# A hybrid encoder on one core: the low half of the attention keys above 64 rows of zeros

## The chip, the cores and the metric

The kernel runs on one core of one Trainium2 chip. The metric is the device time of one execution in microseconds (us). TensorE (PE in the rows) multiplies; its weight loads are listed apart (PEld). VectorE (DVE), ScalarE (ACT) and GpSimd (POOL) work element by element, SyncE (SP) and ScalarE issue transfers. The times before are the median of three runs.

## The reference

An encoder of four layers on 256 tokens of 1024 features, in float32. Each layer is a mixer and an MLP, each behind an RMS norm; the mixers are a state-space mixer (layers 0 and 3), a dilated attention (layer 1) and a differential attention (layer 2). What concerns the change are the attention scores, products of queries and keys over 64 features:

```python
# layer 1, three groups of window and dilation, 16 heads of 64 features
scores = jnp.einsum('brjqhe,brjkhe->brjhqk', qs, kb) / math.sqrt(hd)
scores = jnp.where(valid[:, None], scores + bias, NEG_INF)
...
# layer 2, 8 heads of two halves of 64 features; softmax of each, and their difference
logits = jnp.einsum('bqhie,bkhie->bhiqk', qb, k) + bias
a = jax.nn.softmax(logits, axis=-1)
attn = a[:, :, 0] - lam_full * a[:, :, 1]
```

## The kernel before

Tokens lie along the columns, features along the 128 partitions. Every float32 operand of a large product is split into a high half `hi`, rounded for TensorE's fast format, and a low half `lo`, the rest. A product is then the sum of three: hi x hi, hi x lo, lo x hi (`mm3`, lines 143 to 145). Weights stream from memory in chunks of 1024 columns; ScalarE makes `whi` (line 110) and VectorE `wlo` (line 112), some chunks ahead of their use.

Products over 64 features leave half of the partitions free. `mm2` (lines 128 to 131) uses that: `q` holds the queries' hi in partitions 0 to 63 and their lo in 64 to 127, `kh` holds the keys' hi twice, so that the first product gives hi x hi + lo x hi in one. The second product is hi x lo with the 64 rows of `kl`, the keys' lo:

```python
mm(out, lhsT=q, rhs=kh, start=start, stop=False, skip_group_check=True)
mm(out, lhsT=q[0:64], rhs=kl, start=False, stop=True, skip_group_check=True)
```

`split_keys` (lines 133 to 136) fills `kh` twice by ScalarE and `kl` by VectorE.

The dilated mixer (`dil_events`) runs over 8 head pairs. For each it projects queries and keys of three groups (`qk`), then the values (`vchunk`), and for two blocks of 128 queries makes the scores (`scores`), the transposes (`trans`) and the products with the values (`pv`). Only group 0 uses `mm2`, for the two heads of a pair in turn: four products for a pair and a query block. Groups 1 and 2 use `mm3` with 128 rows: their key tiles hold one head's 64 rows in each half of the columns and zeros elsewhere, written once by POOL.

The differential mixer (`diff_events`) runs over 4 pairs of heads: projections `q`, `k`, `v` (`proj`), then for each head and query block the scores of its two halves by `mm2`, again four products, the softmaxes and their difference `S` on VectorE and ScalarE, transposes (line 1016), the product with the values (line 1028, bank `a3`), a norm of the head whose result `o` is read out of that bank by VectorE (line 1035), and another transpose (line 1042).

Both mixers are lists of events with a time each; the program is emitted in the order of those times, and engines take their instructions in that order. At the start of a mixer stands the norm: POOL adds six of the squares (line 240), TensorE sums them over the features (line 268), in its queue between the first projections.

Of the kernel before, what the change touches and what calls it, by code (L numbers as in the profile page):

```python
# [10 lines left out]
F32 = mybir.dt.float32  # L11
F32R = mybir.dt.float32r
# [4 lines left out]
P = 128  # L17
T = 256
# [12 lines left out]
def classes(t):  # L31
    """Tokens j*4 + c of [.., 256] as [.., c, j]: the order of the dilated mixer."""
    return t.rearrange("p (j c) -> p c j", c=4)


class LayerPool:
    """The pool of the part that is being emitted."""
# [8 lines left out]
class Prog:  # L46
# [20 lines left out]
    @contextmanager  # L67
    def shifted(self, name):
        """Emits with the priority of a later (or earlier) place in the program."""
        n = max(self.tune[name], -self.tc.cur_priority)  # L70
        self.tc.cur_priority += n
        yield
        self.tc.cur_priority -= n

# [5 lines left out]
    def plan_chunk(self, key, ap):  # L80
        """A key that ends in "f32" is used as it is, without a split."""
        self.plan.append((key, ap))
# [44 lines left out]
    def mm2(self, out, q, kh, kl, start):  # L127
        """The product of 64 rows: q holds hi above lo, kh twice the keys' hi."""
        mm = self.nc.tensor.matmul
        mm(out, lhsT=q, rhs=kh, start=start, stop=False, skip_group_check=True)  # L130
        mm(out, lhsT=q[0:64], rhs=kl, start=False, stop=True, skip_group_check=True)  # L131
# [16 lines left out]
    def load(self, g, perm):  # L148
        """x to [feature, token] with the first gains, what the first products need ahead of the other constants."""
# [99 lines left out]
    def rsqrt(self, v, n):  # L249
        """1/sqrt(v) for v [128, n] (the guard within): a seed of the bits and two Newton steps, each with the factors that even its error out."""  # L250
        nc = self.nc
        t = lambda nm, dt=F32: self.ap_.tile([P, n], dt, tag=f"rs_{nm}_{n}", name=f"rs_{nm}_{n}", bufs=2)
        y, w, q = t("y"), t("w"), t("q", I32)
        nc.vector.tensor_scalar(out=q, in0=v.bitcast(I32), scalar1=-0.5, scalar2=float(0x5F1FFFF9), op0=ALU.mult, op1=ALU.add)
        cur = q.bitcast(F32)
        for a, b in ((0.703952253 * 2.38924456, 0.703952253), (1.5 * (1 + 3.17e-7), 0.5 * (1 + 3.17e-7))):
            nc.vector.scalar_tensor_tensor(out=w, in0=cur, scalar=-b, in1=cur, op0=ALU.mult, op1=ALU.mult)
            nc.vector.tensor_tensor(out=w, in0=w, in1=v, op=ALU.mult)
            nc.vector.scalar_tensor_tensor(out=y, in0=w, scalar=a, in1=cur, op0=ALU.add, op1=ALU.mult)
            cur = y  # L260
        return y

    def sums(self, bank, tiles, count):
        """bank [128 tokens, 2 blocks] = sums over the features of each [128 features, 256 tokens] over count, and eps."""
# [6 lines left out]
    def bcast_tok(self, r, scale, bank, out):  # L271
        """r [128 tokens, 2 blocks] times scale -> out [128, 256], the same on every partition."""
# [15 lines left out]
    def normalised(self, g_mix, perm=False, keep=False):  # L288
        """x*g/rms split, all of it."""
# [87 lines left out]
    def tail_chunks(self, key, w, k0, nk):  # L377
        """The last nk row blocks of an output product, cut by columns."""
# [3 lines left out]
    def proj_tail(self, acc, key, xs, finish, first=False):  # L382
        """The last row blocks of an output product, column block by column block."""
# [14 lines left out]
    def ssd_events(self, l, finish):  # L398
        """The layer as (time, weight chunks, emitter); a unit of time is one product of two column blocks."""
# [11 lines left out]
        def start():  # L411
            self.norm_finish("a0")
            st["n"] = self.normalised(gvec("g_mix", 8 * l, 8), keep=any(n[0] != "o" for n in cfg["native"]))
            # sums of squares of the gated y, two column blocks at a time
# [8 lines left out]
        def unit(kind, c0, defer):  # L423
            """Two column blocks of in_w from column c0; -> (bank, keys)."""
# [54 lines left out]
        # dt: softplus, its logarithm, sums along the tokens within the blocks of 128  # L479
# [12 lines left out]
        def dt_post():  # L492
# [24 lines left out]
            # ln(dt): a seed of the bits and Newton steps with exp  # L517
# [8 lines left out]
        def dt_sums():  # L526
            adt, ln = st["adt"], st["ln"]
            b = self.bank("r2")
            ge, le = self.C("tri_ge"), self.C("tri_le")  # [s, s']: 1 where s >= s', s <= s'
# [24 lines left out]
        def load_rows(g, i):  # L554
            """The rows of two heads on every partition."""
# [11 lines left out]
        def cb(g):  # L567
            b = self.bank("r2")
            B, C = st["B", g], st["C", g]
            for i in range(2):  # token blocks 1, 0  # L570
# [15 lines left out]
        def gh(g, i):  # L586
            """The decayed scores of two heads, [s, l] for both directions."""
            bc, tb = st["bc", g, i], st["tb"]
            X = lambda o, i_, bias: nc.scalar.activation(out=o, in_=i_, func=AF.Exp, bias=bias)  # L589
            # blocks of 128: [s1 l0 | s1 l1 | s0 l0 | s0 l1], then the forward diagonals of token blocks 1 and 0  # L590
# [15 lines left out]
        def y(g):  # L606
# [3 lines left out]
            # two heads in turn: they hold different columns of the array  # L610
# [40 lines left out]
        def r2():  # L651
            bank = self.bank("r2")
            # the sums are of 2y
# [52 lines left out]
    def bias_vectors(self):  # L706
        """[16 heads: by k-q from -256 | the same, far ones masked | by (k-q)/4 from -64 | the same, every fourth]."""
# [16 lines left out]
    def bias_rows(self):  # L724
        """Copies of the vectors one after another, of which a slanted pattern reads Toeplitz matrices."""
# [6 lines left out]
    def slanted(self, name, h, off, dims):  # L732
        """Row h of the vectors at off - step*i for each (step, count) of dims, and so on."""
# [4 lines left out]
    def split(self, hi, lo, src, scale):  # L738
        """hi + lo = src*scale, src in PSUM or SBUF."""
# [4 lines left out]
    def dil_events(self, l, finish):  # L744
# [9 lines left out]
        def start():  # L754
# [4 lines left out]
            for i in range(2):  # L759
                st["bias", i] = lp.tile([P, 2, 514], F32, name=f"bias{i}")  # L760
                nc.gpsimd.memset(st["bias", i][:, :, 258:514], -1e30)
                for g in range(1, 3):
# [14 lines left out]
        def qk(hp, g, defer):  # L777
# [15 lines left out]
            if g == 0:  # L793
                q, kh, kl = (lp.tile([P if i < 2 else 64, 2, T], F32R, tag=f"q0{i}", name=f"q0{i}", bufs=2) for i in range(3))
                for h in range(2):
                    r = slice(64 * h, 64 * h + 64)
                    self.split(q[0:64, h, :], q[64:128, h, :], src[r, 0, :], 0.125)
                    self.split_keys(classes(kh[0:64, h, :]), classes(kh[64:128, h, :]), classes(kl[:, h, :]), cj(src[r, 1, :]))
# [73 lines left out]
        def pv(hp, qb):  # L872
            """The two heads in turn: they hold different columns of the array."""
# [46 lines left out]
    def diff_events(self, l, finish):  # L920
# [8 lines left out]
        def start():  # L929
            self.norm_finish("a0")  # L930
            st["n"] = self.normalised(self.V("g_mix", 8 * l, 8))
            # -lambda on every partition; the gain of the head norm with its factor
# [7 lines left out]
            st["nlam"] = t[:, 4:5]  # L940
            nc.vector.tensor_scalar(out=t[:, 5:6], in0=self.V("subln", j), scalar1=1.0 - lam_init, scalar2=None, op0=ALU.mult)
# [8 lines left out]
        def proj(kind, p, defer):  # L950
# [34 lines left out]
            else:  # L985
                st["k", p] = []
                for s_ in range(2):
                    kh, kl = (lp.tile([n, 2, T], F32R, tag=f"k{s_}{n}", name=f"k{s_}{n}", bufs=2) for n in (P, 64))
                    self.split_keys(kh[0:64], kh[64:128], kl, src[64 * s_:64 * s_ + 64])
# [94 lines left out]
    def final_tile(self, n):  # L1084
        """A feature block of x*g, transposed."""
# [42 lines left out]
    def prepare_part(self, i):  # L1128
        """Plans the weights of a part; -> its emitter."""
# [49 lines left out]
def bucket(rel):  # L1179
    """The bucket of each distance (of the shapes alone)."""  # L1180
# [6 lines left out]
def prepare(nc, ins):  # L1187
    """The arrays of the launch: the inputs, laid out, and constants of the shapes alone."""
# [73 lines left out]
```

## Time and profile before

| | us |
|---|---|
| median of three runs | 1647.09 |
| the three runs | 1642.84, 1647.09, 1648.29 |
| span of the profiled execution | 1641.6 |
| dilated mixer within it | 437 to 736 |
| differential mixer within it | 915 to 1045 |

The span goes from the first to the last instruction of one profiled execution; a time of a run also holds what lies around it. Of the profiled execution only the span is recorded. The profile gives, for each engine, how long it was busy; for each stage the same; for each instruction its start and its duration. A matmul's start is observed, its end is modelled, and the next may start long before it.

### The profile page before, as it was taken

The numbers are of one execution on the slowest core, as the hardware profiler recorded it, in microseconds if no ns is written. First come the engines' busy times: TensorE is split into PE (matmuls) and PEld (weight loads), VectorE is DVE, ScalarE is ACT, GpSimd is POOL, SyncE is SP. The second block draws the span as 40 slices with busy tenths as digits, with TensorE's granted clock in tenths as the row PEclk, the third lists the DMA queues.
The fourth block names the chain that finished last, engine by engine and source line by source line (L and its number), as shares of the span: only waits on it lengthen the run. The fifth ranks groups of instructions, "written<-read, shape, count | busy, mean of one in ns | idle before, by whom it ended". The sixth has DMA issues, their size and how long they took to land.

```text
span 1641.6 us, 32376 instructions
## 1 busy us (share of the span) xinstructions
PE 1612.2 (98%) x13018; PEld 1552.6 (95%) x13018; DVE 1198.2 (73%) x1996; ACT 959.9 (58%) x1627; POOL 129.2 (8%) x116
## 2 busy tenths in 40 slices
PE   8999999999999999999999999999999999999998
PEld 7989999999999999999999999999999899899997
DVE  7999997555776666666556888755579999985554
ACT  5577865444666666655445666644455778654443
POOL 0011121000200000010000000100010231210001
PEclk9999999999999999999999999999999999999999
DMA  6677765766475555546665554566655777656651
GB/s 208 209 217 231 224 191 180 218 212 185 134 198 166 151 157 154 161 134 186 190 192 182 184 174 120 166 192 188 187 160 178 218 218 224 217 169 191 187 188 64
DMA packets 230294, 299.84 MB, mean 183 GB/s; under 512 B 16496, under 2 KB 166256, under 8 KB 230144
## 3 DMA queue, kind: packets, MB, share of 16 engines
q1 hardware_dynamic: 209552, 262.51, 52.4%
q10 hardware_dynamic: 20592, 35.27, 7.6%
q8 instruction: 102, 1.67, 0.4%
q14 instruction: 48, 0.39, 0.1%
HBM read 296.41 MB, written 3.62 MB: 183 GB/s over the span
## 4 chain that ended last, share of the span: by engine, by line
PE 79%; DVE 11%; DMA 4%; ACT 3%; issue 2%; POOL 0%; SPq 0%; DVEq 0%; ACTq 0%; POOLq 0%
PE r L143 14%; PE r L145 13%; PE r L144 13%; PE a L143 8%; PE a L145 8%; PE a L144 8%; DVE wlo L112 3%; DMA bc<-scr 2%; DMA raw<-in_ssd_in_w_dram 2%; PE r L141 1%; PE a L820 1%; PE r L614 1%; PE a L822 1%; PE a L821 1%; PE r L131 1%
## 5 line engine op out<-in xcount | busy, mean ns | idle before, releaser
L112 DVE TENSOR_TENSOR wlo<-raw,whi 128x1024 fp32r<-128x1024 f32 (+1 forms) x490 | 593.8, 1219 | 304.7 <-ACT whi L110 303.3
L110 ACT CAST whi<-raw 128x1024 fp32r<-128x1024 f32 (+1 forms) x490 | 502.6, 1032 | 458.1 <-PE r L144 237.6
L145 PE MATMUL r<-spl,wlo 128*128 128x256 f32 x1248 | 356.6, 286 | 3.7 <-DVE wlo L112 3.7
L143 PE MATMUL r<-spl,whi 128*128 128x256 f32 x1248 | 357.4, 287 | 0.5 <-ACT whi L110 0.5
L144 PE MATMUL r<-spl,whi 128*128 128x256 f32 x1248 | 357.3, 286 | 0.3 <-DVE spl L227 0.3
L143 PE MATMUL r<-nh,whi 128*128 128x256 f32 (+1 forms) x1024 | 290.1, 283 | 3.9 <-DVE cvx L469 2.4
L145 PE MATMUL r<-nh,wlo 128*128 128x256 f32 (+1 forms) x1024 | 285.0, 278 | 1.9 <-DVE wlo L112 1.9
L144 PE MATMUL r<-nl,whi 128*128 128x256 f32 (+1 forms) x1024 | 285.0, 278 | 0.0
L143 PE MATMUL a<-hh,whi 128*128 128x256 f32 x1024 | 283.2, 277 | 0.0
L144 PE MATMUL a<-hl,whi 128*128 128x256 f32 x1024 | 283.1, 276 | 0.0
L145 PE MATMUL a<-hh,wlo 128*128 128x256 f32 x1024 | 282.5, 276 | 0.0
L145 PEld LDWEIGHTS r<-spl,wlo 128*128 128x128 f32 x1248 | 242.1, 194 | 4.1 <-DVE wlo L112 3.9
L143 PEld LDWEIGHTS r<-spl,whi 128*128 128x128 f32 x1248 | 242.0, 194 | 1.1 <-ACT whi L110 0.7
L144 PEld LDWEIGHTS r<-spl,whi 128*128 128x128 f32 x1248 | 241.8, 194 | 0.9 <-DVE spl L227 0.5
L143 PEld LDWEIGHTS r<-nh,whi 128*128 128x128 f32 (+1 forms) x1024 | 192.3, 188 | 8.2 <-issue 3.6
L145 PEld LDWEIGHTS r<-nh,wlo 128*128 128x128 f32 (+1 forms) x1024 | 192.4, 188 | 2.8 <-DVE wlo L112 2.1
L144 PEld LDWEIGHTS r<-nl,whi 128*128 128x128 f32 (+1 forms) x1024 | 192.4, 188 | 0.7 <-DVE nl L300 0.2
L143 PEld LDWEIGHTS a<-hh,whi 128*128 128x128 f32 x1024 | 192.4, 188 | 0.2 <-ACT whi L110 0.2
L144 PEld LDWEIGHTS a<-hl,whi 128*128 128x128 f32 x1024 | 192.4, 188 | 0.0
L145 PEld LDWEIGHTS a<-hh,wlo 128*128 128x128 f32 x1024 | 192.2, 188 | 0.0
L240 POOL TENSOR_TENSOR sqacc<-sqacc,sq 128x256 f32<-128x256 f32 x48 | 43.5, 906 | 1129.5 <-ACT sq L238 1126.2
L589 ACT ACTIVATE e<-bc,tb 128x256 f32<-128x256 f32 (+1 forms) x256 | 95.6, 447 | 1.9 <-DVE bc L564 1.4
(250 smaller groups left out, 2421.7 us busy)
## 6 DMA issues: line engine op xcount, KB each, us to landing
raw<-in_mlp_w_dram SPq DMA_DIRECT2D x256, 512.0 KB
raw<-in_ssd_in_w_dram SPq DMA_DIRECT2D x96, 512.0 KB
bc<-scr ACTq DMA_DIRECT2D x32, 768.0 KB
raw<-in_dil_qkv_w_dram SPq DMA_DIRECT2D x48, 512.0 KB
raw<-in_ssd_out_w_dram SPq DMA_DIRECT2D x32, 512.0 KB
raw<-in_dil_qkv_w_dram SPq DMA_DIRECT2D x64, 192.0 KB
raw<-in_diff_qkv_w_dram SPq DMA_DIRECT2D x24, 512.0 KB
raw<-in_dil_out_w_dram SPq DMA_DIRECT2D x8, 512.0 KB
```

The source lines that it names most:

```text
L110: self.nc.scalar.copy(out=hi[:, :n], in_=raw[:, :n])
L112: self.nc.vector.tensor_tensor(out=lo[:, :n], in0=raw[:, :n], in1=hi[:, :n].bitcast(F32), op=ALU.subtract)
L131: mm(out, lhsT=q[0:64], rhs=kl, start=False, stop=True, skip_group_check=True)
L141: mm(out, lhsT=wh, rhs=xh, start=start, stop=stop, skip_group_check=True)
L143: mm(out, lhsT=wh, rhs=xh, start=start, stop=False, skip_group_check=True)
L144: mm(out, lhsT=wh, rhs=xl, start=False, stop=False, skip_group_check=True)
L145: mm(out, lhsT=wl, rhs=xh, start=False, stop=stop, skip_group_check=True)
L240: nc.gpsimd.tensor_tensor(out=self.sqs[0], in0=self.sqs[0], in1=sq, op=ALU.add)
L589: X = lambda o, i_, bias: nc.scalar.activation(out=o, in_=i_, func=AF.Exp, bias=bias)
L614: nc.tensor.matmul(b[(h % 2) * 64:(h % 2) * 64 + 64, n * T:(n + 1) * T], lhsT=xt[:, 1 - i, h * 64:(h + 1) * 64], rhs=G[h][:, i * T:(i + 1) ...
L820: mm(o, lhsT=nh[:, k, t], rhs=w_h, start=k == 0, stop=False)
L821: mm(o, lhsT=nh[:, k, t], rhs=w_l, start=False, stop=False)
```

## The change

The low half of the keys becomes a tile of 128 partitions of which the lower 64 (64 to 127) are zeros, and the second product of `mm2` takes all 128 rows of `q`: q.hi x k.lo + q.lo x 0. The zeros are written once, by POOL, when the mixer starts. So these tiles can't come from a rotating tag any more: the dilated mixer has two standing ones (head pairs alternate), the differential mixer four (two halves, pairs alternate). Before, each had two buffers to a tag, of the same columns.

```diff
@@ mm2
-        mm(out, lhsT=q[0:64], rhs=kl, start=False, stop=True, skip_group_check=True)
+        mm(out, lhsT=q, rhs=kl, start=False, stop=True, skip_group_check=True)
+
+    def lo_keys(self, name):
+        t = self.lp.tile([P, 2, T], F32R, name=name)
+        self.nc.gpsimd.memset(t[64:128].bitcast(F32), 0.0)
+        return t
@@ dil_events, start, for i in range(2)
+                st["kl", i] = self.lo_keys(f"kl{i}")
@@ dil_events, qk
-                q, kh, kl = (lp.tile([P if i < 2 else 64, 2, T], F32R, tag=f"q0{i}", name=f"q0{i}", bufs=2) for i in range(3))
+                q, kh = (lp.tile([P, 2, T], F32R, tag=f"q0{i}", name=f"q0{i}", bufs=2) for i in range(2))
+                kl = st["kl", hp % 2]
...
-                    self.split_keys(classes(kh[0:64, h, :]), classes(kh[64:128, h, :]), classes(kl[:, h, :]), cj(src[r, 1, :]))
+                    self.split_keys(classes(kh[0:64, h, :]), classes(kh[64:128, h, :]), classes(kl[0:64, h, :]), cj(src[r, 1, :]))
@@ diff_events, start
+            for i in range(4):
+                st["kl", i] = self.lo_keys(f"kl{i}")
@@ diff_events, proj
-                    kh, kl = (lp.tile([n, 2, T], F32R, tag=f"k{s_}{n}", name=f"k{s_}{n}", bufs=2) for n in (P, 64))
-                    self.split_keys(kh[0:64], kh[64:128], kl, src[64 * s_:64 * s_ + 64])
+                    kh, kl = lp.tile([P, 2, T], F32R, tag=f"k{s_}", name=f"k{s_}", bufs=2), st["kl", 2 * (p % 2) + s_]
+                    self.split_keys(kh[0:64], kh[64:128], kl[0:64], src[64 * s_:64 * s_ + 64])
```

The rest of the difference takes comments and docstrings out, which shifts line numbers: from `mm3` on, a line has 6 more (line 143 becomes 149), and in the differential mixer 10 more (line 1035 becomes 1045).

On TensorE, the first scores of the dilated mixer before. `r` is the bank of group 0 and then that of groups 1 and 2; of the names behind the arrow the first is the streamed operand, `q_5317` the queries' tile, `q_5318` and `q_5319` the keys' hi and lo, which shared its naming:

```order
L145 MATMUL r_5559<-nh,wlo 128x256
L130 MATMUL r_5635<-q_5318,q_5317 128x256
L131 MATMUL r_5635<-q_5319,q_5317 128x256
L130 MATMUL r_5635<-q_5318,q_5317 128x256
L131 MATMUL r_5635<-q_5319,q_5317 128x256
L143 MATMUL r_5636<-k_5219,q_5393 128x256
```

The same place on TensorE after:

```order
L151 MATMUL r_5562<-nh,wlo 128x256
L130 MATMUL r_5637<-q_5322,q_5321 128x256
L131 MATMUL r_5637<-kl_5219,q_5321 128x256
L130 MATMUL r_5637<-q_5322,q_5321 128x256
L131 MATMUL r_5637<-kl_5219,q_5321 128x256
L149 MATMUL r_5638<-k_5221,q_5396 128x256
```

Nothing moved here: the second product reads another tile, and its rows, which this list doesn't show, are 128 where they were 64.

On POOL, from the last memsets of the dilated mixer over the sums of squares that follow (those of four norms in one row) to the last state-space mixer, before:

```order
L766 MEMSET k_5239 64x256
L765 MEMSET k_5240 64x256
L766 MEMSET k_5240 64x256
L240 TENSOR_TENSOR sqacc<-sqacc,sq 128x256 x24
L600 TENSOR_TENSOR e<-e 128x2x256 x5
```

and after:

```order
L772 MEMSET k_5244 64x256
L773 MEMSET k_5244 64x256
L246 TENSOR_TENSOR sqacc<-sqacc,sq 128x256 x11
L136 MEMSET kl_10952 64x512
L136 MEMSET kl_10954 64x512
L136 MEMSET kl_10956 64x512
L136 MEMSET kl_10958 64x512
L246 TENSOR_TENSOR sqacc<-sqacc,sq 128x256 x13
```

The four memsets of the differential mixer stand ahead of the last of the six adds of its norm. In the dilated mixer's start two memsets of 64x512 join those that stood there, and the last add there has moved up by one place among them: one 64x512 and four 64x256 stand between the first memset of `bias` and it, where six 64x256 stood.

## Rows read from the trace of the kernel before

**Rows 1.** The page's first part: busy time of each engine, its share of the span, its instructions.

```profile
PE 1612.2 (98%) x13018; PEld 1552.6 (95%) x13018; DVE 1198.2 (73%) x1996; ACT 959.9 (58%) x1627; POOL 129.2 (8%) x116
```

**Rows 2.** Busy time by stage, the dilated and the differential mixer. Columns: from and to, length, then busy time (and instructions) of PE, PEld, DVE, ACT and POOL, the granted clock of PE, the busy share of the DMA engines and GB/s.

```profile
437.00:736.00 299.00, 297.77 (x2352) 283.49 (x2352) 204.65 (x431) 189.17 (x333) 9.17 (x16) 0.99 0.55 155
915.00:1045.00 130.00, 129.59 (x1001) 120.90 (x1000) 109.17 (x318) 88.51 (x200) 5.55 (x6) 1.00 0.50 152
```

**Rows 3.** Whom TensorE waited for, from 430 to 736 us and from 905 to 1045 us: us in total, times, the longest.

```profile
PE a L268 <- POOL sqacc L240: 2.4, 1, 2.4
PE r L143 <- DVE q L136: 1.2, 1, 1.2
...
PE a L937 <- DVE lamt L935: 1.7, 1, 1.7
PE a L1042 <- DVE o L1035: 0.4, 2, 0.2
PE a L268 <- POOL sqacc L240: 0.3, 1, 0.3
```

**Rows 4.** The 64-row products of line 131, by their operands (`q,q` in the dilated, `k,q` in the differential mixer), with the least, median and greatest duration in ns, the first and the last start; and the group of 128-row scores of line 144 in the dilated mixer, with its busy time and mean ns.

```profile
L131 PE MATMUL r<-q,q x32: 379/382/382, 469.1 to 698.6; 64*128 64x256 f32 x32
L131 PE MATMUL r<-k,q x32: 380/383/384, 935.4 to 1008.9; 64*128 64x256 f32 x32
...
L144 PE MATMUL r<-k,q 128*128 128x256 f32 x32 | 9.0, 282 | 0.0
```

**Rows 5.** TensorE's timeline at a score of the dilated mixer: start, duration, line, tiles, rows*columns of the weights, the streamed operand.

```profile
468.79 0.28 PE L145 MATMUL r<-nh,wlo 128*128 128x256 f32 x1
468.91 0.28 PE L130 MATMUL r<-q,q 128*128 128x256 f32 x1
469.12 0.38 PE L131 MATMUL r<-q,q 64*128 64x256 f32 x1
469.43 0.38 PE L130 MATMUL r<-q,q 128*128 128x256 f32 x1
469.74 0.38 PE L131 MATMUL r<-q,q 64*128 64x256 f32 x1
470.06 0.39 PE L143 MATMUL r<-k,q 128*128 128x256 f32 x1
470.28 0.28 PE L144 MATMUL r<-k,q 128*128 128x256 f32 x1
470.39 0.28 PE L145 MATMUL r<-k,q 128*128 128x256 f32 x1
470.51 0.28 PE L143 MATMUL r<-k,q 128*128 128x256 f32 x1
```

**Rows 6.** The same at eight score products of the differential mixer, the first two, the last, and what follows.

```profile
982.37 0.28 PE L130 MATMUL r<-k,q 128*128 128x256 f32 x1
982.58 0.38 PE L131 MATMUL r<-k,q 64*128 64x256 f32 x1
...
984.45 0.38 PE L131 MATMUL r<-k,q 64*128 64x256 f32 x1
984.76 0.44 PE L1042 MATMUL a<-head,o 128*128 128x128 f32 x2
```

**Rows 7.** POOL's timeline at the start of the dilated and of the differential mixer: start, duration, what; in brackets the idle time ahead.

```profile
433.20 0.52 POOL L761 MEMSET bias<- 128x512 f32 x1
433.66 0.30 POOL L765 MEMSET k<- 64x256 f32 x1
434.00 0.31 POOL L766 MEMSET k<- 64x256 f32 x1
...
435.76 0.82 POOL L240 TENSOR_TENSOR sqacc<-sqacc,sq 128x256 f32<-128x256 f32 x1
...
906.86 1.94 POOL L240 TENSOR_TENSOR sqacc<-sqacc,sq 128x256 f32<-128x256 f32 x2 [1.61 <-ACT sq L238]
910.41 1.19 POOL L240 TENSOR_TENSOR sqacc<-sqacc,sq 128x256 f32<-128x256 f32 x1 [1.60 <-ACT sq L238]
```

**Rows 8.** Busy time of two head pairs of the differential mixer, columns as in rows 2.

```profile
941.90:966.50 24.60, 24.60 (x191) 22.54 (x190) 19.72 (x60) 17.33 (x40) 0.00 (x0) 1.00 0.59 176
966.50:991.10 24.60, 24.60 (x191) 22.54 (x190) 21.58 (x71) 17.64 (x42) 0.00 (x0) 1.00 0.57 176
```

**Rows 9.** Timelines of VectorE and TensorE where bank `a3` is used again: VectorE's reading of one head (two instructions), then the first product of the next.

```profile
974.98 0.61 DVE L1035 TENSOR_SCALAR o<-a,rs_y 128x128 f32<-128x128 f32 x2
...
976.01 1.05 PE L1028 MATMUL a<-v,PT 128*128 128x128 f32 x8
...
999.35 0.60 DVE L1035 TENSOR_SCALAR o<-a,rs_y 128x128 f32<-128x128 f32 x2
...
1000.72 0.49 PE L1028 MATMUL a<-v,PT 128*128 128x128 f32 x3
```

**Rows 10.** Busy time by stretch as in rows 2, ahead of the first projections of the dilated mixer and behind: the granted clock is the number behind POOL's.

```profile
433.50:437.00 3.50, 0.87 (x6) 0.67 (x6) 3.47 (x6) 2.03 (x4) 3.18 (x10) 1.00 0.36 103
438.00:441.60 3.60, 3.60 (x19) 3.60 (x19) 2.83 (x10) 1.05 (x1) 2.19 (x8) 0.53 0.23 58
```

## The prediction

> **What bounds the kernel now.** I read the busy time by engine first: TensorE is busy 98% of the 1641.6 us span, VectorE 73%, ScalarE 58%, POOL 8% [rows 1]. That is an average over nine stages, so next I cut the two stages that the change touches out of it. The dilated mixer lies between 437 and 736 us, the differential mixer between 915 and 1045 us. In the first TensorE is busy 297.8 of 299 us and VectorE 204.7; in the second TensorE is busy 129.6 of 130 us and VectorE 109.2, which is 84% and much closer [rows 2]. The list of waits says the same: TensorE stands still for 3.6 us (2.4 and 1.2) around the first and 2.4 us around the second, most of it at their starts (the sum of squares, the factor lambda), and none of it at a score [rows 3]. So both mixers are as long as TensorE's row of products, and a product that starts sooner moves all that follows. But a busy TensorE is not yet a TensorE at its pace, since the ends of products are modelled. What counts is the time from one start to the next, which only the timeline shows.
>
> **The products of the scores.** A score takes two products, one with 128 rows (line 130) and one with 64 rows (line 131); there are 64 of the second, 32 in each mixer, recorded at 0.38 us each, where the 128-row product of the same block of scores (line 144) is recorded at 0.28 us [rows 4]. The starts in the dilated mixer tell more [rows 5]. Before the scores, starts lie 0.12 us apart (468.79, 468.91). Then the distances are 0.21 to the first 64-row product, 0.31, 0.31 and 0.32 from one to the next, and 0.22 even from the first 128-row product behind them to the second. After that it is 0.11 or 0.12 again. From 468.91 to 470.28 five distances take 1.37 us. It is not the 64-row product alone that is slow: the 128-row product of line 130 that stands between two of them starts 0.31 late as well, and so does the first product behind them. Each change between 64 and 128 rows costs, in both directions. In the differential mixer the scores of two query blocks often stand in one row of eight, from 982.37 to 984.76: 2.39 us for eight distances [rows 6].
>
> The control for "after" stands in the same rows: lines 143 to 145 `r<-k,q` are scores too, with 128 rows of which half are zeros in the keys, the same shape of 256 columns and the same kind of output. They start 0.115 to 0.12 us apart. The first and second of them (lines 143 and 144) share their weights as the two products of line 130 and 131 do, so that repeated weights are no cost either.
>
> **The change part by part.**
>
> *The product with 128 rows.* With kl 128 rows tall nothing changes its row count any more. Dilated mixer: 1.37 - 5 x 0.117 = 0.785 us for each of 16 blocks (8 head pairs x 2 query blocks), 12.6 us. Differential mixer: 2.39 - 8 x 0.117 = 1.45 us for a row of eight, which is two of its 16 blocks; 8 x 1.45 = 11.6 us. Gross gain 24.2 us. Bounds: nothing at all, if the new products keep 0.31 us, and 24.2 us.
>
> *What takes it back in the dilated mixer.* TensorE being sooner helps only if its inputs are there. Each score still precedes its own softmax, so VectorE and ScalarE are also released sooner; VectorE is busy 68% and ScalarE 63% there [rows 2], and only 0.785 us of some 19 us (299 / 16) are taken out. I take 0, at most 3 us.
>
> *What takes it back in the differential mixer.* Here two head pairs take 49.2 us, with VectorE busy 19.7 + 21.6 = 41.3 us [rows 8]. Four rows of eight fall into that time, so TensorE would want 4 x 1.45 = 5.8 us less, 43.4 us, and VectorE would be 95% busy. The narrow place is the output bank a3: the product of line 1028 must wait until VectorE (line 1035) has read the head before. At 976.01 that reading has been over for 0.42 us (974.98 + 0.61), at 1000.72 for 0.77 us (999.35 + 0.60) [rows 9]. In both cases a row of eight scores lies between the bank's filling and this reuse, so TensorE arrives 1.45 us sooner, and VectorE's part between is a chain that the scores hardly start: TensorE waits about 1.0 and 0.7 us. At the mixer's end, where the last heads run out and no projection is left to hide them, I add 0.6 us by the same reasoning (an estimate from these two rows). Together 2.3 us. Bounds: 0, and 11.6 us if VectorE's present idle time is all latency that can't shrink.
>
> *The memsets.* Six rectangles of 64x512 zeros are added on POOL. A memset of 64x256 takes 0.30 us with the next start 0.35 later, one of 128x512 takes 0.52 with the next 0.46 later [rows 7], so I bound one by 0.35 and 0.52. In the differential mixer all four stand between the fifth and the sixth add of the sum of squares; POOL is free there from 908.80 to 910.41, 1.61 us [rows 7], against 1.4 to 2.1 us for the four. The sixth add starts between 0 and 0.5 us later, and TensorE, which waited 0.3 us for it [rows 3], may wait that much more; I take 0.2. What the first memset waits for are tiles of earlier stages whose readers have long finished. In the dilated mixer the opposite happens: ahead of the sixth add stood six memsets of 64x256 (433.66 to 435.76, 2.10 us), and now stand one 64x512 and four 64x256, 1.75 to 1.9 us. TensorE waits 2.4 us for that add [rows 3], so 0.2 to 0.3 us come back. The two cancel: 0.
>
> *Nothing else moves.* The other engines' orders are as before except for the name of the written tile. The low halves are written by the same VectorE instruction with the same 64 rows, and two (four) standing tiles alternate as the two buffers of each tag did. Weight loads have the same 128 columns.
>
> Sum: 24.2 - 2.3 = 21.9, rounded to 22 us. The profiled execution has a span of 1641.6 us, so its span should become about 1619.6. The median of the three runs, 1647.1 us, lies 5.5 us above that span and the fastest run 1.2 us; I keep the 5.5 and predict 1647.1 - 22 = 1625.1 us.
>
> **The rivals.**
>
> *Nothing is taken back.* VectorE's chains are started by the scores and come sooner by as much. For it: the narrow places are few. Against: 0.42 and 0.77 us of room for 1.45. Then 1647.1 - 24.2 = 1622.9.
>
> *VectorE becomes the bound of the differential mixer.* For it: 84% busy, 95% wanted. Against: its work for weights runs many products ahead, so it has a reserve, and the stage has only four head pairs to use it up. Then only 12.6 us remain: 1634.5.
>
> *The product isn't shortened.* If the 0.31 us belonged to the second use of the array for a score, whatever its rows, nothing would be gained and the time would be 1647. Against it stands the control of [rows 5]: 128-row scores with half their keys zero at 0.12 us. The Trainium skill, page "TensorE: Matmul & The Clock Gate", section "Why this matters for your kernels", says that a single product with few rows takes the same time as one with 128; by that rule alone rows of zeros buy nothing and the sum is 0. The page "TensorEngine Tiling (Array Packing)", section "Key Properties", says that a change of the tiling mode drains the array, without a price; by that, the sum is the one above. From the rows alone: 0.31 us stand only on either side of a 64-row product, 0.12 us between 128-row products of scores, so I leave this rival little.
>
> *Slower: the clock.* Place: the differential mixer's reuse of a3, once per head. When TensorE had been busy only 0.87 of 3.5 us ahead of 437.0, the granted clock stood at 0.53 in the following 3.6 us [rows 10], that is mostly at 1.2 GHz of 2.4, which costs about 1.7 us beside the wait of 2.4 us [rows 3]. If TensorE came to wait as long for VectorE at a head, that head would cost 4.1 us. From six of eight heads on the change is a loss (24.6 against 24.2 us); with all eight, 32.8 us, the time is 1655.7. Against: I expect waits of 1 us, two of them.
>
> **How the numbers follow.** My forecast, part of the gain taken back, 0.57: 1625.1. Nothing taken back 0.25: 1622.9. VectorE bounds the second mixer 0.11: 1634.5. Not shortened 0.05: 1647. Slower by the clock 0.02: 1655.7. The range takes in the first two with the scatter of the runs, which lie 4.3 us below and 1.2 us above their median, and up to some 8 us taken back: 1619 to 1633. A difference under 0.3%, 5 us, can't be told from no change. Faster by more than that 0.93, within it 0.05, slower 0.02.
>
> **What would show it.** In the new profile, the starts around lines 130 and 131 should lie 0.115 to 0.12 us apart with no slow product behind them, and both forms should be recorded at 0.28 us. The dilated mixer should be some 12 us shorter, the differential one some 9. TensorE should show new waits for VectorE's line 1035 (now 1045), of about 1 us, and its wait for the sum of squares should shrink a little in the dilated and grow a little in the differential mixer. I am wrong if the starts keep 0.31 us, or if TensorE's new waits in the differential mixer add up to more than 5 us.

## The result and the profile after

The changed kernel takes 1625.1 us (median of four executions, 1624.6 to 1627.2), the kernel before 1645.0 (four executions, 1641.0 to 1648.3, the three that were known among them). The ratio is 0.9883, with a 95% interval from 0.9866 to 0.9899: 1.2% or 19.8 us faster. Forecast were 1625.1 us, and 22 us less than before. The agreement to 0.1 us is partly luck: the median of before came out 2.1 us lower, and the gain 2 us smaller. The span of the profiled execution, forecast at 1619.6 us, is 1625.4 us: the 5.5 us between a span and the median that the forecast carried over didn't come back.

The busy times by engine are the answer to [rows 1]. TensorE lost 17.7 us of busy time with as many instructions; POOL has the six memsets more.

```profile
PE 1594.5 (98%) x13018; PEld 1550.6 (95%) x13018; DVE 1194.8 (74%) x1996; ACT 959.2 (59%) x1627; POOL 132.9 (8%) x122
```

TensorE's timeline at the score of [rows 5], after:

```profile
466.07 0.28 PE L151 MATMUL r<-nh,wlo 128*128 128x256 f32 x1
466.19 0.28 PE L130 MATMUL r<-q,q 128*128 128x256 f32 x1
466.30 0.28 PE L131 MATMUL r<-kl,q 128*128 128x256 f32 x1
466.42 0.28 PE L130 MATMUL r<-q,q 128*128 128x256 f32 x1
466.54 0.28 PE L131 MATMUL r<-kl,q 128*128 128x256 f32 x1
466.65 0.28 PE L149 MATMUL r<-k,q 128*128 128x256 f32 x1
466.77 0.28 PE L150 MATMUL r<-k,q 128*128 128x256 f32 x1
```

Every distance is 0.11 or 0.12 us; from the first product of the score to the second behind it (466.19 to 466.77) five distances take 0.58 us, where they took 1.37. The row of eight of [rows 6], its first two products, the last, and what follows:

```profile
969.88 0.28 PE L130 MATMUL r<-k,q 128*128 128x256 f32 x1
970.00 0.28 PE L131 MATMUL r<-kl,q 128*128 128x256 f32 x1
...
970.72 0.28 PE L131 MATMUL r<-kl,q 128*128 128x256 f32 x1
970.84 0.38 PE L1052 MATMUL a<-head,o 128*128 128x128 f32 x2
```

0.96 us for eight distances, where it was 2.39. All 64 products are now as in the group of line 131 (answering to [rows 4]; least, median, greatest in ns):

```profile
L131 PE MATMUL r<-kl,q x64: 274/282/363, 466.3 to 991.1; 128*128 128x256 f32 x64
```

Both mixers by windows between the same products as in [rows 2], columns as there:

```profile
433.40:727.40 294.00, 290.26 (x2352) 284.26 (x2353) 204.65 (x431) 189.47 (x333) 10.34 (x19) 0.98 0.56 158
907.10:1026.80 119.70, 118.11 (x999) 117.09 (x999) 108.12 (x317) 87.58 (x200) 5.56 (x6) 0.99 0.55 165
```

The differential mixer is 10.3 us shorter, the dilated only 5.0, though its 16 blocks of scores gave what was forecast. The list of TensorE's waits there (answering to [rows 3]; us in total, times, longest) shows the largest part of what took it:

```profile
PE r L149 <- DVE kl L142: 3.7, 1, 3.7
PE a L274 <- POOL sqacc L246: 2.4, 1, 2.4
...
PE a L1038 <- DVE o L1045: 1.1, 2, 0.7
PE a L1052 <- DVE o L1045: 0.4, 2, 0.2
PE a L274 <- POOL sqacc L246: 0.2, 1, 0.2
```

TensorE waited 1.2 us for the low half of the keys in the first head pair, and now waits 3.7. (The product that waits is a projection: its bank `r` is free only when VectorE has made `kl` out of it. This is called the wait for the low keys from here on.) TensorE's timeline at that wait (idle time ahead in brackets), and the window of what follows, with the granted clock behind PE to POOL:

```profile
472.89 0.28 PE L151 MATMUL r<-nh,wlo 128*128 128x256 f32 x1
476.91 0.55 PE L149 MATMUL r<-nh,whi 128*128 128x256 f32 x1 [3.74 <-DVE kl L142]
477.26 0.42 PE L150 MATMUL r<-nl,whi 128*128 128x256 f32 x1
477.48 0.41 PE L151 MATMUL r<-nh,wlo 128*128 128x256 f32 x1
```

```profile
476.10:482.90 6.80, 5.99 (x28) 6.02 (x29) 3.38 (x7) 3.67 (x9) 0.00 (x0) 0.50 0.76 218
```

A product starts 0.21 us behind the last instead of 0.12: the clock stands at 0.50, that is 1.2 GHz, for 6.8 us. Behind the same wait of before it stood at 1.00:

```profile
478.00:485.00 7.00, 7.00 (x55) 6.48 (x56) 4.45 (x9) 4.66 (x9) 0.00 (x0) 1.00 0.69 194
```

Both kernels have the same products in the same order on TensorE, so each start can be set against its like. The table is worked out from the starts of the two profiled executions (us):

```
before   after    difference  place
 429.1    425.4    -3.7       ahead of the dilated mixer
 465.4    462.7    -2.7       ahead of its first score
 481.9    483.6    +1.8       behind the wait and the slow clock
 707.4    698.8    -8.6       behind its last score
 897.1    888.4    -8.6       ahead of the differential mixer
 927.9    920.6    -7.3       ahead of its first score
1013.3    995.1   -18.2       behind its last score
1200.0   1181.9   -18.2       ahead of the next mixer
1227.1   1210.5   -16.6       behind its start
1621.4   1605.2   -16.2       at the end
```

Each of the 16 blocks of the dilated mixer takes 0.78 us off the difference, and the differential mixer 10.9 us in all. In between, the steps upwards are the first head pair (+5.3 with its one block of -0.8 counted apart: 2.5 of wait, 2.8 of slow clock), three stage starts (+1.0, +1.3, +1.6) and some 1.3 us within the dilated mixer: from 481.9 to 707.4 us 15 blocks should give 11.7 us, and the difference moves by 10.4. These are lost, 0.4 us each, in three stretches of projections that hold no wait (502 to 515, 567 to 581 and 633 to 646 us of before): equal products with 128 rows start 0.114 us apart there before, and 0.118 after. At the three stage starts the clock fell in both kernels, for 3.4 us in this execution of before and for 6.8 in this one of after; the table's first line, 3.7 us ahead of anything that was changed, is scatter of the same kind the other way. So one pair of traces gives the mechanism; the size of the whole has to come from medians, and that of a stretch without such a start from several profiles.

### The profile page after: what moved, and what is told of

The parts are those of the page before. It is cut to its first block, busy times and chain, and to the rows that moved or that the text cites. A ratio compares the mean times of both kernels' runs of the same rounds, so it can differ in the third digit from the quotient of the medians.

```text
span 1625.4 us, 32385 instructions
## 1 busy us (share of the span) xinstructions
PE 1594.5 (98%) x13018; PEld 1550.6 (95%) x13018; DVE 1194.8 (74%) x1996; ACT 959.2 (59%) x1627; POOL 132.9 (8%) x122
## 4 chain that ended last, share of the span: by engine, by line
PE 80%; DVE 10%; DMA 4%; ACT 3%; issue 2%; POOL 0%; SPq 0%; DVEq 0%; ACTq 0%; POOLq 0%
PE r L149 14%; PE r L151 14%; PE r L150 14%; PE a L149 8%; PE a L150 8%; PE a L151 8%; DVE wlo L112 3%; PE r L147 2%; DMA raw<-in_ssd_in_w_dram 2%; PE a L829 1%; PE a L828 1%; PE a L830 1%; DMA bc<-scr 1%; PE r L620 1%; PE a L887 1%
```

## The experiments

My theory: what is slow is a change between 64 and 128 rows, and it costs 0.785 us a block in the dilated mixer and 0.725 in the differential (half of 1.45). Rivals: a 64-row product is slow by itself; the new tiles and memsets have a part in it. On the missing part of the dilated mixer there were two theories: that sooner scores meet VectorE's unchanged chain (the gain turns into the wait), and that the weights of that stretch came late in this execution, whatever the scores.

**The kernel once more.** No edit. From here on, a time is a median, and stands against executions of before on the same chip.

> The changed kernel as it is, a second time. In its profile the first head pair of the dilated mixer waited 3.7 us for VectorE's kl (1.2 us in the kernel before) and the granted clock then stood at half for 6.8 us; at three stage starts it stood at half for 6.8 us where the kernel before had 3.4. Theory: the gain of the scores is fixed (24 us), and what is taken back in the dilated mixer hangs on how late the weights of the first head pair arrive, so that it differs from run to run: a gain of 18 to 22 us again, and a wait of 1 to 4 us at that place. Rival: the wait and the fall of the clock belong to the changed order of POOL and to the sooner scores, and come back in the same size and at the same place in every profile.

1626.4 us against 1645.5, ratio 0.9887 (0.9864 to 0.9910). The gain repeats: 19 to 20 us. The wait for the low keys was 3.5 us and the clock fell behind it again, for 3.4 us.

**Short product.** The tall tiles and the memsets stay, the second product reads 64 rows of them:

```diff
-        mm(out, lhsT=q, rhs=kl, start=False, stop=True, skip_group_check=True)
+        mm(out, lhsT=q[0:64], rhs=kl[0:64], start=False, stop=True, skip_group_check=True)
```

> The changed kernel with its second product taken back to 64 rows; standing tiles and memsets stay. Theory: tiles and memsets cost nothing, so the time is that of the kernel before, within 2 us, and the starts at the scores are 0.21, 0.31, 0.31, 0.32 and 0.22 us apart again. Rival: the memsets on POOL cost time at the two norms, 0.5 to 2 us above the kernel before.

1643.1 us against 1645.5, ratio 0.9985 (0.9972 to 0.9998). Without the 128 rows most of the gain is gone: the changed kernel is 16.6 us faster than this one. The interval leaves tiles and memsets a gain of 0.0 to 0.3%: they cost nothing that can be seen. That this kernel is 2.4 us under before, a little more than the 2 us expected, shows nowhere in the two mixers: from the first score of the one to the last of the other its starts keep within 0.3 us of those of before. TensorE's wait for the sum of squares in the differential mixer is 0.2 us here, with four memsets ahead of it, as it was 0.3 without them.

**One mixer at a time.** The second product has 128 rows in one mixer and 64 in the other (`mm2` gets an argument `tall`, which one of its two callers passes as False):

```diff
+        if tall:
             mm(out, lhsT=q, rhs=kl, start=False, stop=True, skip_group_check=True)
+        else:
+            mm(out, lhsT=q[0:64], rhs=kl[0:64], start=False, stop=True, skip_group_check=True)
```

The dilated mixer alone:

> 128 rows for the second product in the dilated mixer alone. Theory: 16 blocks of 0.785 us, 12.6 us, less what the first head pair takes back (0 to 4.5 us): 8 to 12.6 us faster than before. Rival, that the dilated mixer is bound by its weights and gives nothing: 0 to 2 us.

The differential mixer alone:

> 128 rows for the second product in the differential mixer alone. Theory: 11.6 to 12.3 us of starts less 1.1 us of waits for bank a3 at lines 1028 of the kernel before: 10 to 11 us faster than before. Rival, that VectorE bounds this mixer: under 5 us, with waits of TensorE for VectorE of over 5 us in the differential mixer.

1634.4 us (ratio 0.9937, 0.9916 to 0.9958) and 1633.7 us (0.9932, 0.9911 to 0.9952) against 1645.5: 11.1 and 11.9 us, the second above the 10 to 11 expected. Both rivals have fallen. The sum, 23 us, is more than the 19 to 20 of the whole, but within these intervals (some 3.5 us to either side for each); they are too wide to split the whole exactly. The differential mixer alone shows the two waits at `a3` as the whole change does (1.1 us), and no longer wait in the dilated mixer (1.4 us); the dilated mixer alone shows 3.2 us there, and the slow clock behind it.

**64 rows, in pairs.** Both 128-row products of a block first, then both 64-row products: the same four products, with two changes of the row count where there were four.

```diff
+    def mm22(self, ops):
+        mm = self.nc.tensor.matmul
+        for i, (out, q, kh, kl) in enumerate(ops):
+            mm(out, lhsT=q, rhs=kh, start=i == 0, stop=False, skip_group_check=True)
+        for out, q, kh, kl in ops:
+            mm(out, lhsT=q[0:64], rhs=kl[0:64], start=False, stop=True, skip_group_check=True)
```

> 64 rows for the second product again, but the four products of a block in another order: both with 128 rows first, then both with 64, so that a block changes its rows twice where the kernel before changes four times. Theory, that each change of the rows costs: the distances are 0.12 between the two 128-row products, 0.21 to the first 64-row product, 0.12 between the two 64-row products, 0.31 and 0.22 at the way back, 0.98 us for five where the kernel before has 1.37 and the changed one 0.59; over 32 blocks about 12 us faster than before, half of the gain. Rival, that a 64-row product itself takes 0.31 us: 0.31 between the two 64-row products, some 6 us faster than before.

1634.1 us against 1645.7, ratio 0.9929 (0.9903 to 0.9955): 11.7 us, about half of the 24 us gross for half the changes, with not one zero row added to a product. In the trace a block of the dilated mixer gains 0.39 us, where the changed kernel gains 0.78. TensorE's timeline there (x2: two products in one line):

```profile
470.25 0.28 PE L158 MATMUL r<-nh,wlo 128*128 128x256 f32 x1
470.37 0.40 PE L136 MATMUL r<-q,q 128*128 128x256 f32 x2
470.69 0.50 PE L138 MATMUL r<-kl,q 64*128 64x256 f32 x2
471.12 0.39 PE L156 MATMUL r<-k,q 128*128 128x256 f32 x1
471.34 0.28 PE L157 MATMUL r<-k,q 128*128 128x256 f32 x1
```

Product by product the distances are 0.119 us between the two with 128 rows, 0.208 to the first with 64, 0.223 from that to the second, 0.206 back to 128 rows, 0.223 to the next. A change thus shows in two distances, the one that leads to it and the one behind: 0.208 + 0.223 - 2 x 0.118 = 0.195 us. Four of them are 0.78, the block's price before. That the second 64-row product should already start 0.12 behind the first was wrong; the sum was right.

**64 rows, six in a row.** As above, but the 64-row products are issued three times over, so that the low part counts three times:

```diff
+        for n in range(3):
+            for out, q, kh, kl in ops:
+                mm(out, lhsT=q[0:64], rhs=kl[0:64], start=False, stop=n == 2, skip_group_check=True)
```

> As the kernel with both 128-row products first and both 64-row products behind, but the 64-row products are issued three times over, so that six stand in a row; the low part is thus added three times to the scores. What does a 64-row product cost among its like? Theory, that only the change of rows costs: the second distance is 0.22 (the change), the inner ones 0.12; 32 blocks x 4 x 0.118 = 15 us above the kernel with two. Rival, that a 64-row product itself takes 0.22 us: inner distances of 0.22, 28 us above.

1648.2 us against 1643.7, ratio 1.0017 (0.9991 to 1.0044; ratios are of means, and one execution of before took 1660.8 us). That is 14.1 us more than in pairs, or 16.2 if each is set against before on its own chip (+4.6 and -11.7), for 128 more products: 0.11 to 0.13 us each. The timeline (x6: six products):

```profile
468.20 0.40 PE L136 MATMUL r<-q,q 128*128 128x256 f32 x2
468.52 0.97 PE L139 MATMUL r<-kl,q 64*128 64x256 f32 x6
469.42 0.39 PE L157 MATMUL r<-k,q 128*128 128x256 f32 x1
469.65 0.28 PE L158 MATMUL r<-k,q 128*128 128x256 f32 x1
```

From 468.52 to 469.42 six distances take 0.90 us; without 0.223 behind the change and 0.206 ahead of the next, 0.47 is left for four. So a 64-row product among its like starts every 0.118 us, as a 128-row one does. The rival of the slow 64-row product has fallen. What TensorE does at a change of rows (reload, drain or something else) no run here separates.

**The first head pair with 64 rows.** Tall everywhere but there:

```diff
-                self.mm2(A[:, h * T:(h + 1) * T], q[:, h, t], kh[:, h, :], kl[:, h, :], h == 0)
+                self.mm2(A[:, h * T:(h + 1) * T], q[:, h, t], kh[:, h, :], kl[:, h, :], h == 0, hp > 0)
```

> The changed kernel, with 64 rows for the second product in the first head pair of the dilated mixer alone. In three profiles with 128 rows there, TensorE waited 3.2 to 3.7 us for kl behind that pair's first scores and the clock fell; in three profiles with 64 rows it waited 1.2 to 1.4 us. Theory one, that the sooner scores make the wait: the wait is 1.2 to 2.2 us, and the time is that of the changed kernel or up to 2 us less. Theory two, that late weights make it, which landed 1 to 2 us later in those three profiles before any score had run: the wait is anything from 1 to 4 us, whatever the rows of the first pair.

1625.8 us against 1645.7, ratio 0.9877 (0.9842 to 0.9912), and a wait of 2.4 us with the slow clock behind it (for 3.4 us), though the first scores are as slow as before. Theory one had 2.2 at most; sooner scores are not needed for a longer wait.

**The bias earlier.** In the trace of after, transfers of the bias tables (ScalarE's queue) and of the weights (SyncE's) are issued side by side ahead of the first head pair. Here the first pair's tables are issued earlier:

```diff
-            E(t0 + c["bias"], lambda hp=hp: load_bias(hp))
+            E(t0 + c["bias"] if hp else -0.5, lambda hp=hp: load_bias(hp))
```

> The changed kernel, with the bias transfers of the first head pair issued some 6 us sooner on ScalarE's queue, ahead of the run of weight transfers. Theory, that those transfers and the weights share the engines and make the weights late: the wait for kl falls to 2 us or less, no fall of the clock behind it, and the time is 2 to 5 us under that of the changed kernel. Rival, that the weights are late for another reason: wait and time as in the changed kernel, within 2 us.

1626.8 us, ratio 0.9886 (0.9855 to 0.9916): no gain. The wait for the low keys fell to 0.7 us, but TensorE now waited 2.3 us for weights at 454 us, and the clock fell behind that.

**Three more profiles,** of one execution each, on one chip: the kernel before, the short product and the changed kernel.

> The kernel before, another profile. So far the weights behind the first scores of the dilated mixer came early in three profiles, all of kernels whose scores there have 64 rows in the old order, and 1.2 to 1.9 us later in five, four of them with sooner scores and one without. Theory one, chance: early or late here, with a wait of TensorE for the keys' low half of 1.2 to 1.4 us if early and of 2.2 to 2.6 us if late. Theory two, that the kernel decides: early, 1.2 to 1.4 us.

> The changed kernel with 64 rows in the second product, another profile, as the one before: 1.2 to 1.4 us by the kernel, 1.2 to 2.6 us by chance.

> The changed kernel, a third profile. Theory two: late weights and a wait of 3.2 to 3.7 us as in both before. Theory one: late again or early, and if early a wait of 2.0 to 2.2 us (1.2 to 1.4 and the 0.8 by which the first scores are sooner).

The waits for the low keys were 1.0, 1.0 and 2.2 us, the times 1641.0, 1647.7 and 1625.3. So one and the same kernel, the changed one, waits 3.7, 3.5 and 2.2 us in three profiles; 2.2 is what theory one, chance, had for early weights. ScalarE's timeline ahead of the wait, of after as first profiled, three casts of weights and what each waited for:

```profile
460.74 1.05 ACT L110 CAST whi<-raw 128x1024 fp32r<-128x1024 f32 x1 [2.54 <-PE a L830]
...
466.00 1.05 ACT L110 CAST whi<-raw 128x1024 fp32r<-128x1024 f32 x1 [1.55 <-DMA raw<-in_dil_qkv_w_dram]
467.79 1.05 ACT L110 CAST whi<-raw 128x1024 fp32r<-128x1024 f32 x1 [0.75 <-DMA raw<-in_dil_qkv_w_dram]
```

The same three in the third profile of the same kernel, and VectorE's first step of the softmax behind them in it:

```profile
460.98 1.05 ACT L110 CAST whi<-raw 128x1024 fp32r<-128x1024 f32 x1 [1.85 <-DMA raw<-in_dil_qkv_w_dram]
...
465.42 1.05 ACT L110 CAST whi<-raw 128x1024 fp32r<-128x1024 f32 x1 [0.61 <-DMA raw<-in_dil_qkv_w_dram]
467.33 1.05 ACT L110 CAST whi<-raw 128x1024 fp32r<-128x1024 f32 x1 [0.86 <-PE r L150]
469.55 0.61 DVE L856 CUSTOM_DVE_ANT_0 S<-r,bias 128x256 f32<-128x256 f32 x1
```

The second of these executions stood 1.1 us later on TensorE at one product near the mixer's start (441.35 against 440.29), and yet the last two casts start 0.6 and 0.5 us sooner: by each execution's own time the first one's casts are 1.6 and 1.5 us late, and both waited for the DMA of their weights. VectorE carries this on to the wait. In after as first profiled it makes `wlo` of the last of these chunks, then starts the softmax, whose first scores had been issued by 466.7 us, and comes to the low keys at last:

```profile
468.87 1.23 DVE L112 TENSOR_TENSOR wlo<-raw,whi 128x1024 fp32r<-128x1024 f32 x1 [0.57 <-ACT whi L110]
470.01 0.61 DVE L856 CUSTOM_DVE_ANT_0 S<-r,bias 128x256 f32<-128x256 f32 x1
...
476.15 0.62 DVE L142 TENSOR_TENSOR kl<-r,q 64x256 fp32r<-64x256 f32 x1 [0.25 <-ACT q L141]
```

From this step of the softmax to the low keys it takes 6.1 or 6.2 us in all profiles but that with six products in a row, so the end of the wait follows the weights and not the scores. Of all profiles but that with the earlier bias, worked out from the traces (start of the ninth cast, which is the second of those three, in us behind that product of TensorE; the casts of the first 17 us stand alike within 0.2 us, and the first score stands at about 26):

```
execution                     ninth cast  scores of the first pair  wait  slow clock behind it
before, first                 23.8        64 rows                   1.2   no
before, second                23.5        64 rows                   1.0   no
short product, first          23.7        64 rows                   1.4   no
short product, second         23.6        64 rows                   1.0   no
differential mixer alone      23.9        64 rows                   1.4   no
six in a row                  23.8        64 rows, six in a row     1.1   no
changed kernel, third         24.1        128 rows                  2.2   3.4 us
first head pair with 64 rows  24.9        64 rows                   2.4   3.4 us
in pairs                      25.4        64 rows, in pairs         3.0   3.4 us
dilated mixer alone           25.3        128 rows                  3.2   3.4 us
changed kernel, second        25.6        128 rows                  3.5   3.4 us
changed kernel, first         25.7        128 rows                  3.7   6.8 us
```

Both theories hold, each for a part. Sooner scores add about 0.8 to 1.3 us to the wait (1.0 to 1.4 against 2.2 with early weights, 2.4 against 3.2 to 3.7 with late ones), and late weights another 1.0 to 1.5. The weights are late before the first score runs. That the scatter of executions alone can do it is shown by the changed kernel, early once and late twice. Whether they are late more often in some kernels stays open. The kernels of the table's upper six rows were early six times of six, those of the lower six once of six, a lopsided split for chance; yet the edits of the changed kernel, the short product and the kernels with one mixer alone or the first head pair apart leave the work ahead of the first score as it is.

The 0.118 us of the three stretches of projections, for 0.114 before, are no chance: all six profiles with 128 rows in the dilated mixer (the first head pair aside) show them, and none of the seven with 64 rows there. Why, stays open.

## Why the prediction was right, and where it was off

*What bounds the kernel.* Right. TensorE's row of products sets both mixers; what was taken out of it moved all that follows, to the end (-18.2 behind the last score, -16.2 at the end, with a fall of the clock between).

*The product with 128 rows, 24.2 us gross.* Right in place and size: 0.78 us a block (forecast 0.785), 2.39 to 0.96 a row of eight (forecast to 0.94). The reading behind it, that each change between 64 and 128 rows costs in both directions, is shown by the pairs (half the changes, half the gain a block) and by the six in a row (no cost between equal row counts). In the differential mixer the forecast took eight distances of a row of eight and left out the one behind it, which is 0.1 us shorter too where a product of 256 columns follows. The rule of the Trainium skill, page "TensorE: Matmul & The Clock Gate", section "Why this matters for your kernels", that a product with few rows (32 there) takes the same time as one with 128, agrees with the 0.118 us of both; it says nothing of neighbours with another row count, and so the result that it would have given, no gain, did not come. The Trainium skill, page "TensorEngine Tiling (Array Packing)", section "Key Properties", says that a change of the tiling mode drains the array; that would fit the 0.195 us a change, but that a drain is what happens there no run shows.

*What takes it back in the dilated mixer: 0, at most 3 us.* This is the step that was mis-sized. In the profiled execution the mixer gives 5.9 us from its first score to its last, where 12.5 were gained at the scores: 5.3 us were taken back in the first head pair, 2.5 as a longer wait and 2.8 as a slow clock, and 1.3 by the three slower stretches of projections. In the two other profiles of the changed kernel and in that of the dilated mixer alone it gives 7.4 to 8.5 us, so that 4.0 to 6.6 us are taken back in four profiles. The medians agree with that, but loosely: the dilated mixer alone against before leaves 12.6 - 11.1 = 1.5 us, with some 3.5 us to either side, and the step from the differential mixer alone to the whole change 12.6 - 7.2 = 5.4, from executions that lie within 2.4 and 0.6 us. I argued that VectorE and ScalarE, busy 68% and 63% of the mixer, would be released sooner too. As far as TensorE's waits go, that holds for 15 of the 16 blocks. It fails for the first head pair, where [rows 3] had a wait of 1.2 us for the low keys: what ends it is a chain on ScalarE and VectorE whose other input is weights from DMA, and those come no sooner when the scores do. The slower stretches were in no term of the sum.

*What takes it back in the differential mixer: 2.3 us.* The mechanism was right, the size too large. The two waits at `a3` stand where they were forecast:

```profile
963.44 1.13 PE L1038 MATMUL a<-v,PT 128*128 128x128 f32 x8 [0.71 <-DVE o L1045]
...
985.53 1.13 PE L1038 MATMUL a<-v,PT 128*128 128x128 f32 x8 [0.35 <-DVE o L1045]
```

0.71 and 0.35 us, where 1.0 and 0.7 were forecast, and nothing more at the mixer's end, where I had added 0.6 (line 1052 waits 0.4 us, as line 1042 did). Net 10.9 us in the profiled execution (10.8 to 11.0 in five others with 128 rows there) and 11.9 by the medians of that mixer alone, against 9.3.

*The memsets, 0.* Right, shown by the short product. That the wait for the sum of squares would shrink in the dilated mixer by 0.2 to 0.3 us did not show: 2.4 us before and after. The memset of 64x512 that stands there had its next start 0.55 us behind, over the bound of 0.52, and started 0.12 us later behind that of `bias` than the one of 64x256 did, so the add came as late as before. Nor did the wait grow in the differential mixer (0.3 and 0.2 us).

The errors of the two mixers have opposite signs, though the dilated one's is the larger: the gain came out 2 to 3 us short of 22, and the lower median of before made up for it in the time. *The rivals*: the product was shortened; VectorE did not become the differential mixer's bound, and no head cost the clock there; but the mechanism of the slower rival, a wait with a slow clock behind it, did turn up, in one place, in the other mixer.

## What to carry to other kernels

Measure products on TensorE by the distance of starts over the whole neighbourhood, not by the recorded time of the odd one: here a product with 64 rows is as fast among its like as one with 128, and the price is paid at each change, about half of it by the product behind the change. If a short product can be filled with zeros for nothing, fill it; if not, put the short ones together, which halves the price here without a single zero. When a gain on TensorE's row is added up, look first at the waits that are already in the list within the stage, and ask what ends each. A wait that ends with something other than the shortened products, as the one for the low keys ends with weights, swallows what was gained just ahead of it. One whose end moves with them swallows nothing: the wait for lambda at the differential mixer's start is 1.7 us in every profile, whether the dilated mixer ahead of it had become shorter or not.

## What the runs showed of the hardware

- A change of a product's rows between 128 and 64, in either direction, cost 0.195 us in all, spread over the distance that leads to it (0.208 or 0.206 us) and the next one (0.223), where equal neighbours of either kind stood 0.118 us apart.
- Equal 128-row products themselves ran at one of two distances, 0.114 and 0.118 us, for whole stretches at the full clock. Which one a stretch had changed with the row counts of the scores ahead of it in three stretches of the dilated mixer; the cause is open.
- In the first head pair the granted clock fell to 1.2 GHz behind each of six waits of 2.2 to 3.7 us, for 3.4 us five times and 6.8 once, and behind a wait of 2.3 us for weights in the kernel with the earlier bias; it stayed at 2.4 GHz behind each of six waits of 1.0 to 1.4 us. A fall of 3.4 us cost 1.3 to 1.7 us beside the wait (it can begin within the wait).
- At the start of the differential mixer the fall lasted 3.4 us in five of thirteen executions, 6.8 in five and 10.2 in three; one and the same kernel had 3.4 and 10.2 (the short product), or 6.8 and 10.2 (the changed one). At half the clock, that alone scatters the time by up to some 3.4 us.
